# Squared values of the MLP stored unsplit, split on load by ScalarE and GpSimd

## The chip, the cores and the metric

The kernel runs on one core of a Trainium2 chip. The metric is the device time of one execution in microseconds (us), lower is better; runs of one kernel are summarised by their median. The kernel before takes 2271.26 us (median of 3 runs, 2271.02 to 2272.39).

## The reference

One decoder block on an input of 1024 rows by 1024 columns in float32: two token mixers (dilated attention and retention), an output projection, and at the end the MLP that this change is about:

```python
    xn2 = rmsnorm(x, norm2_g[l])
    x = x + jnp.square(jax.nn.relu(xn2 @ w_up[l])) @ w_down[l]
```

`w_up` is 1024 x 4096 and `w_down` 4096 x 1024. All of it is float32.

## The kernel before

**Split products.** Each float32 operand of a matmul is split into a high part, a rounded copy of type fp32r that ScalarE writes (`activation` Copy), and a low part, the rest (`tensor_tensor` subtract on VectorE). The helper `split` does both; its two lines are L318 and L319. Each product is then three matmuls: high by high, high by low, low by high. The function `group` (line L223) issues them all. Only TensorE's order is written out by hand; the order on the other engines comes from a planner that puts instructions in the order in which it expects them to be ready, with expected durations of its own, and each engine then runs its list strictly in order. All transfers are issued from SyncE's queue (SP), in order too.

**Strassen.** Both MLP products use Strassen's scheme in Winograd's form: seven products N1 to N7 in place of eight. TensorE sums them in PSUM banks: bank `a` holds N1 and then N2 added on top, bank `b` holds minus N1 (copied there by ScalarE, L387 and L1163) and then N6, N7 and N4, bank `d` holds N5 and then N3. Between two products of one bank, some engine reads the intermediate sum, and the next product of that bank has to wait for it.

**Up projection.** 16 units j (256 columns of `w_up` each), seven products of 12 matmuls (128x128 by 512 columns) per unit, in the order of `strassen_order`: N6, N5, N1 of unit j+2, N7, N2 of unit j+2, N4, N3. After N7, ScalarE copies bank `b` out (L395), then N4 goes on in that bank. The class `Weights` keeps a fixed list of weight splits; a raw weight buffer is loaded again (L176) as soon as the last split that reads it is done. Each result passes Relu and Square on ScalarE (L1110, L1111). The four squared quarters (`q11`, `q12`, `u3`, `u2`) and four sums of them that VectorE makes (L1117) are the seven left operands of the down projection. `put_operand` splits each of them into `hs` (high and low, 128 x 2 x 512) and stores both parts to `h_d` in DRAM (L1127), 512 KB each.

**Down projection.** 8 chunks c (512 rows of `w_down`) by 4 row blocks t make 32 units u. `load_rows(u)` loads the unit's seven operands, already split, into one of three places that served the up projection (`OP7["N1"]`, `["N5"]`, `["N3"]`): 896 KB of high parts and 896 KB of low parts (L1143). `down(u, name)` is one product of 6 matmuls. The order within a unit is N6, N5, N1 of unit u+1, N7, N2 of unit u+1, N3, N4; after that `load_rows(u + 3)`. VectorE adds or subtracts each sum to the output rows `Y` (L1171). The seven weight operands of the next chunk are made and split while a chunk runs (L153 are the sums on VectorE), most of them around a change of chunk, since their buffers come free there.

**The seam.** The last unit of the up projection overlaps the first two products of the down projection, written by hand:

```python
            if j == NU - 1:
                if name == "N1":
                    load_rows(0)
...
                if name == "N5":
                    load_rows(1)
                if name == "N7":
                    down(0, "N1")
                if name == "N4":
                    down(0, "N2")
                if name == "N3":
                    load_rows(2)
```

Lines and names that come up later: L223 all matmuls (`mm`, `ms` are the PSUM tiles, `xh`, `xl` the high and low operand, `wh`, `wl` those of the weights), L318 and L319 the splits, L1127 the stores of `h_d`, L1143 the row loads, L852 and L332 GpSimd's few small powers in earlier stages.

Of the kernel before, what the change touches and what calls it, by code (L numbers as in the profile page):

```python
# [17 lines left out]
P = 128  # L18
S = 1024
D = 1024  # L20
# [248 lines left out]
def hybrid_block(ctx: ExitStack, tc: tile.TileContext, a: dict, out: bass.AP):  # L269
# [26 lines left out]
    h_d = dram.tile([FF // 512, 2, 4, P, 7, 2, P], F, name="h_d")  # L296
# [60 lines left out]
    for nb in range(2):  # L357
        for u in range(4):
# [6 lines left out]
                  {"N1": "y1a", "N2": "y1b", "N3": "y1c", "N5": 3, "N7": "w1a", "N6": "w1b", "N4": "w1c"}])  # L365
# [720 lines left out]
    with ExitStack() as ph:  # L1086
        up_pool, early, sumst = None, [], ExitStack()
        unit = {}

        def temps():  # L1090

            nonlocal up_pool
            if up_pool is None:
                assert pipe.slot > last_turn
                norm2.close()
                y0 = pool(sumst, "y0", 1)
                Y.update((r, y0.tile([P, D], F, name=f"Y{r}")) for r in (0, 4))
                up_pool = pool(ph, "p26", 2)
            return up_pool

        def result(j, f, cs, src):
# [13 lines left out]
            if q == "u2":  # L1115
                for name, x, y in (("N5", "u3", "u2"), ("N7", "u2", "q11"), ("N6", "q11", "u3"), ("N3", "q12", "q11")):
                    nc.vector.tensor_tensor(held[j, x], held[j, x], held[j, y], op=OP.add)  # L1117
                    put_operand(j, name, held[j, x])
# [3 lines left out]
        def put_operand(j, name, x):  # L1122

            hs = temps().tile([P, 2, 512], R, name="hs", bufs=4)
            split(hs[:, 0], hs[:, 1], x)
            dst = h_d[j // 2, :, :, :, DOWN.index(name), j % 2]
            nc.sync.dma_start(dst.rearrange("h t p q -> p (h t) q"),  # L1127
                              hs.rearrange("p h (t q) -> p (h t) q", q=P).bitcast(F))
# [6 lines left out]

        def load_rows(u):

            if u < len(units):
                c, t = units[u]
                rows[u] = []  # L1140
                for i, x in enumerate(OP7[("N1", "N5", "N3")[u % 3]]):
                    x = x.rearrange("p a b -> p (a b)")[:, :7 * 2 * P]
                    nc.sync.dma_start(x.bitcast(F), h_d[c, i, t].rearrange("p o k q -> p (o k q)"))  # L1143
                    rows[u].append(x.rearrange("p (o k q) -> p o k q", o=7, k=2))

        def down(u, name):
# [9 lines left out]
            xh, xl = rows[u]  # L1156
# [19 lines left out]

        for j, name in strassen_order(NU):
            product("up", j, name, unit, OP7, temps, result)
            if j == NU - 1:
                if name == "N1":  # L1180
                    load_rows(0)
                if name == "N2":
                    parts = [x.rearrange("p a b -> p (a b)") for x in OP7[name]]
                    for i, part in enumerate("ab"):
                        W.places["n2" + part] = [x[:, 1024 * i:1024 * i + 1024] for x in parts]
                    W.free(("place", "n2"))
                if name == "N5":
                    load_rows(1)
                if name == "N7":
                    down(0, "N1")  # L1190
                if name == "N4":
                    down(0, "N2")
                if name == "N3":
                    load_rows(2)
# [3 lines left out]
        Y.update((r, y1.tile([P, D], F, name=f"Y{r}")) for r in (1, 5, 3, 7, 2, 6))  # L1198
        for x in "abc":
            W.places["y1" + x] = [y1.tile([P, UW], R, name=f"y1{x}{i}") for i in "hl"]  # L1200
# [3 lines left out]
    with ExitStack() as ph:  # L1204
# [5 lines left out]
        for u in range(len(units)):  # L1210
            for name, later in (("N6", False), ("N5", False), ("N1", True), ("N7", False), ("N2", True),
# [3 lines left out]
            load_rows(u + 3)  # L1215
# [107 lines left out]
```

## Time and profile before

| | |
|---|---|
| time, median of 3 runs | 2271.26 us |
| profiled execution, its own time | 2274.39 us |
| its span, first to last instruction | 2272.6 us |
| granted TensorE clock, mean | 0.996 |
| TensorE busy | 2233.6 us, 98% |
| VectorE, ScalarE, GpSimd busy | 59%, 44%, 5% |
| up projection | about 1639 to 1950 us of the span |
| down projection | about 1950 us to the end |
| `h_d` traffic: stores; row loads | 112 of 512 KB; 64 of 896 KB |

In the views below, PE is TensorE, DVE VectorE, ACT ScalarE, POOL GpSimd, SP SyncE's queue. A list of waits says which engine and line waited for which, then the total us, the number of times and the longest. A row of the timeline gives start, duration, engine, line, operation, `out<-in` by the program's names, and in brackets the idle time before it with what ended it. A row of a group gives count, busy us, mean ns of one, and the idle time before. The chain of waits is the chain of work that ended last, followed back to what released each step. Matmuls overlap, so their pace is read from start to start, not from their durations.

### The profile page before, as it was taken

The page shows a single profiled execution, that of the slowest core. Times are in us where ns is not written, and L with a number is a line of the kernel's source. Part 1 is how long each engine was busy: PE and PEld are TensorE (multiplying, and loading weights), DVE is VectorE, ACT ScalarE, POOL GpSimd, SP SyncE. Part 2 cuts the span into 40 slices and gives each one's busy share as a digit, 9 for nine tenths or more (in the row PEclk, how much of TensorE's full clock was granted, in tenths as well). Part 3 has the DMA queues.
Part 4 walks back from the last instruction along what each step waited for, and adds up shares of the span by engine and source line. Part 5 has one row for each costly group of instructions (what it writes and reads, how often), then busy time and mean ns, then how long its engine had stood idle before and what let it go on. Part 6 is the DMA issues. An engine that isn't in the chain of part 4 may idle for free.

```text
span 2272.6 us, 29996 instructions
## 1 busy us (share of the span) xinstructions
PE 2233.6 (98%) x10868; PEld 1911.3 (84%) x10868; DVE 1338.5 (59%) x2580; ACT 992.0 (44%) x2182; POOL 103.3 (5%) x148
## 2 busy tenths in 40 slices
PE   8999999999999999999999999999999999799999
PEld 7999999998888888888888878888787777688887
DVE  6444545455544445558676752363877777777874
ACT  6444435345433333345455633122567667532220
POOL 1111111110000000000000000000000000000000
PEclk9999999999999999999999999999999999899999
DMA  4313132323233333363433385554278888967665
GB/s 148 98 52 107 62 94 86 90 85 98 84 111 109 109 109 112 105 185 119 119 121 95 120 286 181 167 162 161 89 219 239 244 237 265 335 252 287 252 226 201
DMA packets 288805, 353.53 MB, mean 156 GB/s; under 512 B 14609, under 2 KB 215441, under 8 KB 288658
## 3 DMA queue, kind: packets, MB, share of 16 engines
q1 hardware_dynamic: 288658, 351.63, 48.4%
q8 instruction: 85, 1.39, 0.3%
q14 instruction: 62, 0.51, 0.1%
HBM read 229.84 MB, written 121.73 MB: 155 GB/s over the span
## 4 chain that ended last, share of the span: by engine, by line
PE 78%; DVE 8%; DMA 5%; ACT 5%; issue 3%; POOL 0%; SPq 0%; POOLq 0%; DVEq 0%; ACTq 0%
PE mm L223 52%; PE ms L223 20%; DVE wl L319 2%; DMA raw<-in_w_up 2%; PE ms L603 1%; PE ms L583 1%; ACT wh L318 1%; PE tr L659 1%; DVE Y L1171 1%; DVE hs L319 1%; DVE xl L319 1%; PE ms L596 1%; DVE raw L153 1%; ACT u L1110 1%; PE ms L819 1%
## 5 line engine op out<-in xcount | busy, mean ns | idle before, releaser
L223 PE MATMUL mm<-wh,xh 128*128 128x384 f32 (+1 forms) x1280 | 503.4, 393 | 9.3 <-DMA xh<-h_d 9.3
L319 DVE TENSOR_TENSOR wl<-raw,wh 128x1024 fp32r<-128x1024 f32 (+2 forms) x274 | 296.4, 1088 | 303.8 <-ACT wh L318 302.9
L223 PE MATMUL mm<-wh,xl 128*128 128x384 f32 (+1 forms) x1280 | 460.4, 360 | 3.0 <-DVE xl L319 2.0
L223 PE MATMUL mm<-wl,xh 128*128 128x384 f32 (+1 forms) x1280 | 459.3, 359 | 0.0
L318 ACT ACTIVATE wh<-raw 128x1024 fp32r<-128x1024 f32 (+2 forms) x274 | 258.6, 950 | 322.3 <-PE ms L223 81.0
L223 PE MATMUL mm<-xl,wh 128*128 128x512 f32 x848 | 309.8, 390 | 1.7 <-DVE xl L319 1.7
L223 PE MATMUL mm<-xh,wh 128*128 128x512 f32 x848 | 310.3, 390 | 0.0
L223 PE MATMUL mm<-xh,wl 128*128 128x512 f32 x720 | 280.6, 390 | 0.0
L223 PEld LDWEIGHTS mm<-wh,xh 128*128 128x128 f32 x1280 | 242.2, 189 | 30.3 <-ACT w1ch L318 9.7
L223 PEld LDWEIGHTS mm<-wh,xl 128*128 128x128 f32 x1280 | 241.2, 188 | 26.1 <-DVE xl L319 3.0
L223 PEld LDWEIGHTS mm<-wl,xh 128*128 128x128 f32 x1280 | 243.1, 190 | 19.3 <-DVE wl L319 0.4
L223 PE MATMUL ms<-xh,wh 128*128 128x512 f32 x604 | 239.7, 397 | 7.3 <-ACT u L395 4.5
L223 PE MATMUL ms<-xh,wl 128*128 128x512 f32 x604 | 235.4, 390 | 0.0
L223 PE MATMUL ms<-xl,wh 128*128 128x512 f32 x604 | 235.2, 389 | 0.0
L223 PEld LDWEIGHTS mm<-xl,wh 128*128 128x128 f32 x848 | 159.6, 188 | 35.0 <-DVE xl L319 2.1
L223 PEld LDWEIGHTS mm<-xh,wh 128*128 128x128 f32 x848 | 159.6, 188 | 33.2
L223 PEld LDWEIGHTS mm<-xh,wl 128*128 128x128 f32 x720 | 135.4, 188 | 28.2
L223 PEld LDWEIGHTS ms<-xh,wh 128*128 128x128 f32 x604 | 113.5, 188 | 36.9 <-ACT u L395 10.4
L223 PEld LDWEIGHTS ms<-xh,wl 128*128 128x128 f32 x604 | 113.3, 188 | 23.9
L223 PEld LDWEIGHTS ms<-xl,wh 128*128 128x128 f32 x604 | 113.5, 188 | 22.2
L590 ACT ACTIVATE pr<-s,acc 128x128 f32<-128x128 f32 (+1 forms) x96 | 43.1, 449 | 148.7 <-DVE acc L588 124.0
L1171 DVE TENSOR_TENSOR Y<-Y,ms 128x512 f32<-128x512 f32 x88 | 60.3, 685 | 62.5 <-PE ms L223 62.3
(257 smaller groups left out, 3295.0 us busy)
## 6 DMA issues: line engine op xcount, KB each, us to landing
h_d<-hs SPq DMA_DIRECT2D x112, 512.0 KB, 5.1
xh<-h_d SPq DMA_DIRECT2D x32, 896.0 KB, 5.0
xl<-h_d SPq DMA_DIRECT2D x32, 896.0 KB, 7.2
raw<-in_w_att SPq DMA_DIRECT2D x48, 384.0 KB, 3.9
raw<-in_w_up SPq DMA_DIRECT2D x32, 512.0 KB, 4.2
raw<-in_w_down SPq DMA_DIRECT2D x32, 512.0 KB, 5.5
sg_d<-sg SPq DMA_DIRECT2D x32, 256.0 KB, 2.0
raw<-in_w_rqk_q SPq DMA_DIRECT2D x16, 512.0 KB, 3.7
```

The costliest lines, as they stand in the source:

```text
L153: self.nc.vector.tensor_tensor(self.raw[r], self.raw[r], self.raw[other], op=op)
L223: self.nc.tensor.matmul(ps, x, y, start=start, stop=stop, skip_group_check=not first)
L318: nc.scalar.activation(dst_h, src, AF.Copy)
L319: nc.vector.tensor_tensor(dst_l, src, dst_h.bitcast(F), op=OP.subtract)
L583: nc.tensor.matmul(sp[:, :n], qT[:, b * P:(b + 1) * P], kT[:, k0:k0 + n], start=True, stop=True)
L590: nc.scalar.activation(st["p"][:, :n], s[:, :n], AF.Exp, bias=acc[:, b, DH:DH + 1], accum_out=acc[:, b, DH + 1:DH + 2])
L596: nc.tensor.transpose(tp[:, j * P:(j + 1) * P], st["p"][:, j * P:(j + 1) * P], ident)
L603: nc.tensor.matmul(po[:, :DH], st["t"][:, j * P:(j + 1) * P], V[:, k0 // P + j, :], start=(j == 0), stop=(j == nk - 1))
L659: nc.tensor.transpose(pt[:, j, :], qk[:, j, :], ident)
L819: nc.tensor.matmul(sp[:, :P], kT[:, f], qT[:, f], start=(f == 0), stop=(f == 1))
L1110: nc.scalar.activation(r, src, AF.Relu)
L1171: nc.vector.tensor_tensor(Y[r][:, ns], Y[r][:, ns], ps, op=op)
```

## The change

`h_d` keeps each operand once, unsplit, in float32. `put_operand` stores the squared value or sum as it is, 256 KB; the sums of a unit go into tiles of their own (`s`, four buffers), so that the value being stored isn't overwritten. `hs` and its splits are gone.

The down projection loads a unit's seven operands raw, 896 KB in all, into one of two halves of the place `OP7["N1"]` (`raws`). `split_rows` splits them: ScalarE copies the high parts in one instruction, GpSimd subtracts the low parts in slices of 256 columns, one per operand. The first two operands (N1, N2), which a unit needs one unit ahead, are split on their own into the small pool `rn`; the other five go into one of two places (`row_places`), `OP7["N5"]` and a new pair of tiles in the pool `y1`. `prepare(u)`, now at the start of unit u, splits the five operands of unit u+1, issues the load of unit u+3 and splits the pair of unit u+2. At the seam the rows of units 0 and 1 are asked for after (15, N1) and those of unit 2 after (15, N5). The weight operands N2 and N3 of odd chunks move from `y1` to `OP7["N3"]`, which the rows no longer use.

```diff
--- before.py
+++ after.py
@@ -293,7 +293,7 @@
     pb_d = dram.tile([KT, P, S], F, name="pb_d")
     v_d = dram.tile([HEADS, S, DH], F, name="v_d")
 
-    h_d = dram.tile([FF // 512, 2, 4, P, 7, 2, P], F, name="h_d")
+    h_d = dram.tile([FF // 512, 4, P, 7, 2, P], F, name="h_d")
     y_d = dram.tile([S, D], F, name="y_d")
 
     def slot_of(from_):
@@ -362,7 +362,7 @@
     NC = FF // 512
     W.add_chunks("dn", [[a["w_down"][c, i] for i in range(4)] for c in range(NC)],
                  [{"N1": 0, "N2": 1, "N3": 2, "N5": "n2a", "N7": "n2b", "N6": 5, "N4": 4},
-                  {"N1": "y1a", "N2": "y1b", "N3": "y1c", "N5": 3, "N7": "w1a", "N6": "w1b", "N4": "w1c"}])
+                  {"N1": "y1a", "N2": "n3a", "N3": "n3b", "N5": 3, "N7": "w1a", "N6": "w1b", "N4": "w1c"}])
     pipe = Pipe(nc)
 
     def product(tag, j, name, unit, operands, pu, result):
@@ -1084,7 +1084,7 @@
 
 
     with ExitStack() as ph:
-        up_pool, early, sumst = None, [], ExitStack()
+        up_pool, first_two, early, sumst = None, None, [], ExitStack()
         unit = {}
 
         def temps():
@@ -1095,6 +1095,8 @@
                 norm2.close()
                 y0 = pool(sumst, "y0", 1)
                 Y.update((r, y0.tile([P, D], F, name=f"Y{r}")) for r in (0, 4))
+                nonlocal first_two
+                first_two = pool(sumst, "rn", 2)
                 up_pool = pool(ph, "p26", 2)
             return up_pool
 
@@ -1113,19 +1115,17 @@
             if q != "u2":
                 put_operand(j, {"q11": "N1", "q12": "N2", "u3": "N4"}[q], r)
             if q == "u2":
-                for name, x, y in (("N5", "u3", "u2"), ("N7", "u2", "q11"), ("N6", "q11", "u3"), ("N3", "q12", "q11")):
-                    nc.vector.tensor_tensor(held[j, x], held[j, x], held[j, y], op=OP.add)
-                    put_operand(j, name, held[j, x])
+                for name, x, y in (("N5", "u3", "u2"), ("N7", "u2", "q11"), ("N6", "q11", "N5"), ("N3", "q12", "N6")):
+                    held[j, name] = temps().tile([P, 512], F, name="s", bufs=4)
+                    nc.vector.tensor_tensor(held[j, name], held[j, x], held[j, y], op=OP.add)
+                    put_operand(j, name, held[j, name])
 
         held = {}
 
         def put_operand(j, name, x):
 
-            hs = temps().tile([P, 2, 512], R, name="hs", bufs=4)
-            split(hs[:, 0], hs[:, 1], x)
-            dst = h_d[j // 2, :, :, :, DOWN.index(name), j % 2]
-            nc.sync.dma_start(dst.rearrange("h t p q -> p (h t) q"),
-                              hs.rearrange("p h (t q) -> p (h t) q", q=P).bitcast(F))
+            dst = h_d[j // 2, :, :, DOWN.index(name), j % 2]
+            nc.sync.dma_start(dst.rearrange("t p q -> p t q"), x.rearrange("p (t q) -> p t q", q=P))
 
 
         units = [(c, t) for c in range(NC) for t in range(4)]
@@ -1133,15 +1133,38 @@
         sums = {}
         Y = {}
 
+        def flat(name):
+            return [x.rearrange("p a b -> p (a b)") for x in OP7[name]]
+
+        raws = [x[:, :7 * 2 * P].bitcast(F) for x in flat("N1")]
+        row_places = [[x[:, :5 * 2 * P] for x in flat("N5")]]
+
         def load_rows(u):
 
             if u < len(units):
                 c, t = units[u]
-                rows[u] = []
-                for i, x in enumerate(OP7[("N1", "N5", "N3")[u % 3]]):
-                    x = x.rearrange("p a b -> p (a b)")[:, :7 * 2 * P]
-                    nc.sync.dma_start(x.bitcast(F), h_d[c, i, t].rearrange("p o k q -> p (o k q)"))
-                    rows[u].append(x.rearrange("p (o k q) -> p o k q", o=7, k=2))
+                nc.sync.dma_start(raws[u % 2], h_d[c, t].rearrange("p o k q -> p (o k q)"))
+
+        def split_rows(u, pair):
+
+            if u < len(units):
+                n = 2 if pair else 5
+                if pair:
+                    h, l = (first_two.tile([P, n * 2 * P], R, name=x) for x in ("rh", "rl"))
+                else:
+                    h, l = row_places[u % 2]
+                src = raws[u % 2][:, :512] if pair else raws[u % 2][:, 512:]
+                nc.scalar.activation(h, src, AF.Copy)
+                for i in range(n):
+                    cs = slice(2 * P * i, 2 * P * i + 2 * P)
+                    nc.gpsimd.tensor_tensor(l[:, cs], src[:, cs], h[:, cs].bitcast(F), op=OP.subtract)
+                rows[u, pair] = [x.rearrange("p (o k q) -> p o k q", o=n, k=2) for x in (h, l)]
+
+        def prepare(u):
+
+            split_rows(u + 1, False)
+            load_rows(u + 3)
+            split_rows(u + 2, True)
 
         def down(u, name):
 
@@ -1153,7 +1176,8 @@
                 b[bank] = mm.tile([P, 512], F, name="mm")
             o = DOWN.index(name)
             wh, wl = W["dn", c, name]
-            xh, xl = rows[u]
+            xh, xl = rows[u, o < 2]
+            o = o if o < 2 else o - 2
             pipe.step(b[bank], [(xh[:, o, k], xl[:, o, k], wh[:, 512 * k:512 * k + 512], wl[:, 512 * k:512 * k + 512])
                                 for k in range(2)], None, fresh)
             ps = b[bank]
@@ -1174,30 +1198,37 @@
             if t == 3:
                 W.free(("dn", c, name))
 
+        def weight_places(name, slot):
+
+            for i, part in enumerate("ab"):
+                W.places[name + part] = [x[:, 1024 * i:1024 * i + 1024] for x in flat(slot)]
+            W.free(("place", name))
+
         for j, name in strassen_order(NU):
             product("up", j, name, unit, OP7, temps, result)
-            if j == NU - 1:
-                if name == "N1":
-                    load_rows(0)
-                if name == "N2":
-                    parts = [x.rearrange("p a b -> p (a b)") for x in OP7[name]]
-                    for i, part in enumerate("ab"):
-                        W.places["n2" + part] = [x[:, 1024 * i:1024 * i + 1024] for x in parts]
-                    W.free(("place", "n2"))
-                if name == "N5":
-                    load_rows(1)
-                if name == "N7":
-                    down(0, "N1")
-                if name == "N4":
-                    down(0, "N2")
-                if name == "N3":
-                    load_rows(2)
+            if j < NU - 1:
+                continue
+            if name == "N1":
+                load_rows(0)
+                load_rows(1)
+                split_rows(0, True)
+            if name == "N2":
+                weight_places("n2", name)
+            if name == "N5":
+                prepare(-1)
+            if name == "N7":
+                down(0, "N1")
+            if name == "N4":
+                down(0, "N2")
+            if name == "N3":
+                weight_places("n3", name)
         exts.close()
         y1 = pool(sumst, "y1", 1, "right")
 
-        Y.update((r, y1.tile([P, D], F, name=f"Y{r}")) for r in (1, 5, 3, 7, 2, 6))
-        for x in "abc":
-            W.places["y1" + x] = [y1.tile([P, UW], R, name=f"y1{x}{i}") for i in "hl"]
+        Y.update((r, y1.tile([P, D], F, name=f"Y{r}")) for r in (1, 5))
+        row_places.append([y1.tile([P, 5 * 2 * P], R, name=f"r{x}1") for x in "hl"])
+        W.places["y1a"] = [y1.tile([P, UW], R, name=f"y1a{x}") for x in "hl"]
+        Y.update((r, y1.tile([P, D], F, name=f"Y{r}")) for r in (3, 7, 2, 6))
         W.free(("place", "y1"))
 
 
@@ -1208,11 +1239,11 @@
         W.free(("place", "w1"))
         px = pool(ph, "px7", 2)
         for u in range(len(units)):
+            prepare(u)
             for name, later in (("N6", False), ("N5", False), ("N1", True), ("N7", False), ("N2", True),
                                 ("N3", False), ("N4", False)):
                 if u + later < len(units):
                     down(u + later, name)
-            load_rows(u + 3)
             c, t = units[u]
             if 2 <= c < 6 and t % 2 == 0:
 
```

## The prediction

> **What bounds the kernel now.** I read the page's busy line first, then the windows table by stage, TensorE's list of waits, the timeline of each wait, and last the queues that the change touches.
>
> ```profile
> PE 2233.6 (98%) x10868; PEld 1911.3 (84%) x10868; DVE 1338.5 (59%) x2580; ACT 992.0 (44%) x2182; POOL 103.3 (5%) x148
> ...
> 1639.00:1950.00 311.00, 306.06 (x1325) 248.00 (x1323) 240.61 (x333) 213.41 (x350) 0.00 (x0) 1.00 0.82 239
> 1950.00:1976.00 26.00, 15.10 (x59) 11.62 (x60) 22.39 (x26) 16.39 (x24) 0.00 (x0) 0.81 1.00 336
> 1976.00:2111.00 135.00, 134.76 (x585) 110.48 (x584) 92.73 (x113) 37.03 (x46) 0.00 (x0) 0.99 0.74 272
> 2066.00:2089.00 23.00, 22.95 (x102) 18.61 (x101) 22.68 (x27) 7.53 (x9) 0.00 (x0) 1.00 0.73 256
> ```
>
> The window rows give length, then busy time and count of PE, PEld, DVE, ACT, POOL, then granted clock, DMA share, GB/s. TensorE (PE) sets the time nearly everywhere, and the change leaves its 10868 matmuls and their order alone. So only TensorE's waits can move the time: those that go, and those that come. The first row is the up projection, the second the seam, the third steady down projection, the last one chunk boundary in it. GpSimd (POOL) does nothing in all four. TensorE's waits here:
>
> ```profile
> PE mm L223 <- DMA xh<-h_d: 9.3, 1, 9.3
> ...
> PE ms L223 <- ACT u L395: 4.5, 13, 0.5
> ...
> PE ms L223 <- DVE wl L319: 1.1, 1, 1.1
> PE mm L223 <- DMA xl<-h_d: 0.9, 1, 0.9
> ```
>
> The columns are total us, times, longest. Two sit at the seam and are rows that arrive late, one at the seam is a weight split, and one returns 13 times in the up projection.
>
> **The seam: what goes.**
>
> ```profile
> 1963.17 0.69 DVE hs L319
> ...
> 1964.61 1.56 SPq L1143
> ...
> 1966.22 8.16 DMA xl<-h_d
> 1962.60 0.39 PE L223 MATMUL mm<-xh,xl 128*128 128x512 f32 x1
> 1972.32 0.76 PE L223 MATMUL mm<-wh,xh 128*128 128x512 f32 x1 [9.33 <-DMA xh<-h_d]
> ...
> 1974.42 0.80 PE L223 MATMUL mm<-wh,xl 128*128 128x512 f32 x1 [0.92 <-DMA xl<-h_d]
> ...
> 1979.71 0.42 PE L223 MATMUL mm<-wh,xl 128*128 128x512 f32 x1
> 2037.10 2.72 PE mm L223 x12
> ```
>
> The last row gives the undisturbed pace, 2.72/12 = 0.227 us a matmul. From 1962.60 to 1979.71 TensorE starts 15 matmuls in 17.11 us; at pace they take 3.40. The seam's row wait costs 13.7 us, not the 10.2 of the wait rows: behind the gap the matmuls ran at 0.43 spacing, and the granted clock of that window is 0.81. The cause stands in the first three rows (chain of waits): the rows of unit 2 are issued on SP's queue at 1964.61, behind the last stores, which wait for the low-part split at 1963.17 on VectorE; then the transfer takes 8.16 us with the DMA engines at a share of 1.00.
>
> The change moves that load: unit 2's rows are asked for after the (15,N5) product, in front of the last four stores, and wait only for GpSimd to have read unit 0's rows. It also halves the bytes:
>
> ```profile
> h_d<-hs SPq DMA_DIRECT2D x112, 512.0 KB, 5.1
> xh<-h_d SPq DMA_DIRECT2D x32, 896.0 KB, 5.0
> xl<-h_d SPq DMA_DIRECT2D x32, 896.0 KB, 7.2
> ```
>
> The 112 stores become 256 KB each, the 64 row loads 32: 28.7 + 28.7 MB fewer. I take the 13.7 us as gone. What is late next is the split of the rows: unit 1's five operands need a place that an earlier product frees, one ScalarE copy and five GpSimd subtractions, all by the start of unit 1, and unit 3's load waits for them. I charge 1 us (0 to 7 in the range). The weight split of N6, 1.1 us of wait and some 0.4 of slow restart, goes too, since VectorE loses its `hs` subtractions right ahead of it: 1.5.
>
> **The up projection: what goes.**
>
> ```profile
> 1669.35 4.20 DMA raw<-in_w_up
> ...
> 1885.75 4.28 DMA raw<-in_w_up
> 1884.51 1.22 DVE L319 TENSOR_TENSOR wl<-raw,wh 128x1024 fp32r<-128x1024 f32 x1
> 1890.06 2.01 ACT L318 ACTIVATE wh<-raw 128x1024 fp32r<-128x1024 f32 x2 [0.83 <-DMA raw<-in_w_up]
> 1891.97 0.58 ACT L395 ACTIVATE u<-ms 128x512 f32<-128x512 f32 x1
> 1892.60 0.50 PE L223 MATMUL ms<-xh,wh 128*128 128x512 f32 x1 [0.46 <-ACT u L395]
> L318 ACT ACTIVATE hs<-q 128x512 fp32r<-128x512 f32 x64 | 40.0, 625 | 33.7 <-DVE q L1117 29.9 <-DMA h_d<-hs 3.3
> L319 DVE TENSOR_TENSOR hs<-q,hs 128x512 fp32r<-128x512 f32 x64 | 43.8, 688 | 5.2 <-ACT hs L318 5.2
> ```
>
> The first two rows are eleven units apart: 19.67 us a unit, where 84 matmuls at pace take 19.04. So 0.63 a unit is lost, 8.2 over the 13. It is a loop: a weight buffer frees when VectorE's split ends (1885.73), its load lands 4.28 later, ScalarE, which stood idle 0.83 for it, makes two 1.0 us copies and only then the copy L395 that N4 needs. The change takes 7 `hs` copies (0.63) off ScalarE and 7 subtractions (0.69) off VectorE per unit, 4.4 and 4.8 us; at least one pair is in each round of the chain (about 1.2 us, twice the 0.63), and the DMA share falls from 0.82 by the halved stores. The four additions of a unit stay, only into tiles of their own. Bounds: nothing if the order of ScalarE keeps L395 behind a late load, 8.2 if the loop gets shorter than 19.04; I take 8.2 because the loop needs to shrink by only 3%.
>
> **The down projection: what comes.** Per unit of 42 matmuls (9.52 us): one ScalarE copy of 1280 columns and one of 512, and seven GpSimd subtractions of 128x256 (224 in all). ScalarE: 1024 columns take about 1.05 (a 1.05 to 1.06 row stands in the up group's 2.01 for two), 512 take 0.63, so 1280 about 1.3, with 0.63 makes 1.9 a unit; it is busy 37.03 of 135, so 27% becomes 47%. What is queued behind them is the copy of N1's sum, which N2 waits for one product (1.36 us) later:
>
> ```profile
> L1163 ACT ACTIVATE ms<-mm x30: 578/582/591, 1976.5 to 2256.6; 128x512 f32<-128x512 f32 x30
> ```
>
> That leaves 0.78 us. The long copy is free to run at the unit's start, 4 us earlier; the short one waits for rows that land about then. I charge nothing for it; if it collides, up to 0.5 us a unit.
>
> GpSimd's subtraction has no row. Nearest rows:
>
> ```profile
> L319 DVE TENSOR_TENSOR ql<-rqT,qh x28: 418/426/426, 1005.7 to 1288.6; 128x256 fp32r<-128x256 f32 x28
> L852 POOL TENSOR_TENSOR st<-st,half x32: 549/888/1522, 1015.3 to 1316.9; 128x1 f32<-128x1 f32 x32
> 1261.09 1.52 POOL L852 TENSOR_TENSOR st<-st,half 128x1 f32<-128x1 f32 x1 [10.24 <-DVE st L851]
> 1260.98 1.23 DVE L319 TENSOR_TENSOR xl<-oar,xh 128x1024 fp32r<-128x1024 f32 x1
> ```
>
> VectorE does the same shape in 0.42: the low end. A GpSimd instruction alone has 0.55 even for one column (a power); with VectorE's 0.42 for the columns that is 0.97: the high end. I take T = 0.7, between the two. Seven make 4.9 us of 9.52, so GpSimd isn't the bound below T = 1.36. The Trainium skill (GPSIMD Engine Reference, "Performance versus the Vector engine") gives 4497 ns for a two-tensor add of 2048 columns, about twice VectorE; an eighth of it, 0.56, is an estimate from that page, and no run here shows it; the sum by it would be 2249.
>
> The last two rows show more: 549 ns became 1.52 us where GpSimd started just behind a VectorE operation with two SBUF inputs, and it ended 0.4 after that one. GpSimd waited about 0.97 for VectorE. So the two take turns. At a chunk boundary VectorE has no slack: 22.68 busy of 23.00 in the window row, with twelve two-input operations between these two,
>
> ```profile
> 2066.43 1.22 DVE L319 TENSOR_TENSOR wl<-raw,wh 128x1024 fp32r<-128x1024 f32 x1
> ...
> 2085.75 1.22 DVE L319 TENSOR_TENSOR wl<-raw,wh 128x1024 fp32r<-128x1024 f32 x1
> 2086.88 0.68 DVE L1171 TENSOR_TENSOR Y<-Y,ms 128x512 f32<-128x512 f32 x1
> 2087.48 0.68 DVE L1171 TENSOR_TENSOR Y<-Y,mm 128x512 f32<-128x512 f32 x1
> ```
>
> mostly one `Y` addition apart (0.60 from start to start; its other input is PSUM). A GpSimd turn fits into that 0.60; what is longer delays VectorE, by T - 0.6 each time if VectorE must also wait for GpSimd, which no row shows. The `Y` additions behind are what lets TensorE reuse the bank two products (2.72 us) later. At 0.7 it is 12 x 0.1 = 1.2 a boundary, of which I let half through, and I add 0.4 for rows that GpSimd, with about one turn per VectorE turn, delivers late: 1.0, seven boundaries, 7 us. Ends: nothing (or 2 us of gain, the 0.3 a boundary that TensorE loses there today), and 12 x 0.37 x 7 = 31 at T = 0.97.
>
> SP's queue gets a new wait: the load for unit u+3 waits for GpSimd's subtractions, and weight loads stand behind it. They have a chunk (38 us) of time, so I cost it at nothing; if GpSimd were a whole unit late, weights would be too. Weights placed elsewhere cost nothing: the new place is free after (15,N3), and chunk 1 needs it 28 us later.
>
> **Sum.** -13.7 - 1.5 + 1 - 8.2 + 7 = -15.4. The profiled execution took 2274.39 (span 2272.6 and 1.8 around it), so 2259.0 there; the median of the runs is 3.1 lower, 2271.26, so 2255.9: 2256.
>
> **Rivals.**
> - *Turn-taking decides (slower).* Place: the chunk boundaries. Price: 12 x (T - 0.6) each. From 3.2 a boundary, T = 0.87, the 22.4 of gains are gone; at 0.97 the time is 2271.3 - 22.4 + 31 = 2280. For it: VectorE's full window, and GpSimd's stretched rows. Against: the order alternates with PSUM additions. The Trainium skill (SBUF — State Buffer, "SBUF: two separate sides") says the pair of ports is held exclusively for the whole instruction by a two-SBUF-input VectorE operation or by GpSimd, and the loser blocks; the trace agrees for GpSimd (0.55 to 1.52), the other direction is unseen.
> - *GpSimd is the bound.* Above T = 1.36 each of 31 units lasts 7T: at 1.8, 12.6, so 2271 - 22 + 31 x 3.1 = 2345. Against: its fixed 0.55 and VectorE's rate.
> - *The up projection's loop stays*, since ScalarE's order still puts late weights ahead of L395: 2256 + 8 = 2264.
> - *A new wait at the seam*: unit 1's split or unit 3's rows late by 7 us more: 2263. For it: ScalarE is busy 16.39 of 26 there and VectorE 22.39.
>
> **How the numbers follow.** Forecast 0.55 (own range 2249 to 2264), turns 0.17, GpSimd bound 0.05, loop 0.12, seam 0.11. A measurement can tell about 0.2%, 4.5 us: faster is below 2266.7, slower above 2275.8. Faster: 0.53 + 0.02 + 0.10 + 0.09 = 0.74; same 0.09; slower 0.17. The range: 2246 (nothing lost at boundaries, 2 gained) to 2276, which leaves out most of the turns' end and the GpSimd bound.
>
> **What would show it.** Right: no wait for `h_d` rows at the seam and a granted clock near 1 there; L395 gone from TensorE's waits; 128x256 GpSimd operations near 0.7; DMA share near 0.5 in both projections. Wrong: GpSimd operations over 0.9, TensorE waits on `Y` additions or on the low rows at the boundaries, or ScalarE's L1163 behind a row copy.

## The result, and the profile after

The kernel after takes 2334.01 us (median of 4 runs, 2331.58 to 2337.01) against 2271.82 us of the kernel before in the same comparison (4 runs, 2271.02 to 2273.3): ratio 1.0274, 95% interval 1.0256 to 1.0291. It is slower by 62 us, where 2256 was forecast. The profiled execution took 2336.11 us, its span is 2334.3, which is 61.7 more than the span before.

The windows by stage of the kernel after, in the columns explained in the prediction (the up projection at its pace, up projection with the start of the seam, the window in which the seam of the kernel before lay, and the down projection in two parts):

```profile
1650.00:1930.00 280.00, 280.00 (x1236) 231.56 (x1235) 164.71 (x211) 147.52 (x226) 5.99 (x5) 1.00 0.54 161
1639.00:1950.00 311.00, 307.91 (x1348) 253.69 (x1347) 188.50 (x236) 167.84 (x257) 19.82 (x16) 0.99 0.54 160
1950.00:1976.00 26.00, 24.15 (x105) 19.29 (x104) 14.04 (x16) 14.87 (x22) 13.02 (x16) 0.99 0.72 248
1976.00:2111.00 135.00, 113.75 (x450) 91.05 (x449) 83.69 (x95) 45.63 (x55) 75.28 (x74) 0.90 0.35 127
2111.00:2334.00 223.00, 188.08 (x756) 148.63 (x754) 121.73 (x148) 59.87 (x71) 108.58 (x119) 0.93 0.32 111
```

The up projection is what was forecast: TensorE is busy in all of the 280 us. In the window where the seam of the kernel before lay it is busy for 24.15 of 26 instead of 15.10, but the seam has moved: the down projection now starts at 1939.38 instead of 1949.08, and its unit 0 takes 15.27 us where 9.52 is the pace. The large loss is in the fourth and fifth rows, where before TensorE had 134.76 of 135. No engine is the bound there: VectorE works 83.69 of 135, GpSimd 75.28, ScalarE 45.63, and the DMA share has fallen from 0.74 to 0.35. Low busy shares everywhere with a TensorE that waits are the mark of a chain in which things happen one after another.

By starts of the matmuls, the 61.7 us split so: the down projection starts 9.7 earlier (8.4 of the up projection, 1.3 from ahead of it), units 0 and 1 take 24.79 instead of 34.33 (9.5 gained), and from unit 2 to the last matmul it takes 365.96 instead of 285.01 (81.0 lost). Units 2 to 30 take 12.39 us on the mean instead of 9.60.

The list of waits of the kernel after from 1950 us to the end shows the chain (us in total, times, longest):

```profile
POOL rl L1160 <- ACT rh L1157: 154.0, 34, 6.7
ACT rh L1157 <- DMA xl<-h_d: 113.0, 15, 9.3
ACT rh L1157 <- DMA xh<-h_d: 71.3, 12, 9.2
...
PE ms L223 <- DVE Y L1195: 42.8, 10, 8.3
DVE xl L319 <- ACT xh L318: 32.4, 9, 7.5
...
PE mm L223 <- ACT ms L1187: 10.9, 8, 3.4
```

and SP's own list over the same stretch:

```profile
SPq L1146 <- POOL rl L1160: 83.9, 14, 8.0
...
SPq L1146 <- POOL xl L1160: 64.7, 14, 6.8
```

Read together they close a ring: SP's row load (L1146) waits for GpSimd's subtraction, ScalarE's copy (L1157) waits for the load, GpSimd's subtraction (L1160) waits for the copy. The chain of waits in that stretch goes round it (start, us, what; in the loads `xh` and `xl` are the raw buffers of even and odd units, by the names of the tiles whose places they took; as outputs of L1160, `xl` and `rl` are places of low parts):

```profile
1997.94 5.00 DMA xl<-h_d
...
2003.05 0.64 ACT rh L1157
...
2003.76 1.15 POOL rl L1160 x2
...
2005.16 3.53 POOL xl L1160 x5
...
2008.70 4.47 DMA xh<-h_d
...
2013.28 0.64 ACT rh L1157
...
2013.99 1.15 POOL rl L1160 x2
...
2015.38 5.55 POOL rl L1160 x5
...
2020.95 4.44 DMA xl<-h_d
```

From load to load it is 10.76 and 12.25 us: 4.5 to 5.0 of transfer, 0.64 of copy, 1.4 for the pair's two subtractions, and 3.5 (undisturbed) or 5.5 (beside VectorE) for five subtractions. TensorE needs new rows each 9.52. The five subtractions at 2005.16 read the other buffer (`xl<-xh`), whose rows had lain there all along: in the order that the planner made, GpSimd does the pair of unit u+2 first and then the five of unit u+1, while the next load may start only when those five are done. So the five wait for a load that they don't need. From the seventh row load on, each one starts only after the one before it has landed, 10.2 to 16.7 us after that one's start, 12.7 on the mean: about the 12.39 of a unit.

What the ring does to TensorE goes over two more queues. The timeline of the kernel after around one boundary:

```profile
2025.49 0.63 ACT L1157 ACTIVATE rh<-xl 128x512 fp32r<-128x512 f32 x1 [8.96 <-DMA xl<-h_d]
2026.03 1.04 ACT L318 ACTIVATE xh<-raw 128x1024 fp32r<-128x1024 f32 x1
...
2027.11 1.59 DVE L319 TENSOR_TENSOR xl<-raw,xh 128x1024 fp32r<-128x1024 f32 x1 [6.78 <-ACT xh L318]
2028.62 0.68 DVE L1195 TENSOR_TENSOR Y<-Y,mm 128x512 f32<-128x512 f32 x1
...
2030.54 0.80 PE L223 MATMUL ms<-w1ah,rh 128*128 128x512 f32 x1 [6.16 <-DVE Y L1195]
```

ScalarE stands 8.96 us at the copy of the late rows; behind it in its list is a weight split, VectorE stands 6.78 for that with a `Y` addition behind it, and TensorE waits 6.16 for the bank which that addition should have read. The rows that were late weren't even due: TensorE is at N7 (`w1ah`) of a unit, and this pair is first used by the N1 that runs in the next unit.

### The profile page after: what moved, and what is told of

It reads as the page before. It is cut to its first block, busy times and chain, and to the rows that moved or that the text cites. A ratio compares the mean times of both kernels' runs of the same rounds, so it can differ in the third digit from the quotient of the medians.

```text
span 2334.3 us, 30051 instructions
## 1 busy us (share of the span) xinstructions
PE 2254.4 (97%) x10868; PEld 1925.9 (83%) x10868; DVE 1286.5 (55%) x2468; ACT 987.3 (42%) x2134; POOL 318.8 (14%) x372
## 3 DMA queue, kind: packets, MB, share of 16 engines
q8 instruction: 85, 1.39, 0.2%
## 5 line engine op out<-in xcount | busy, mean ns | idle before, releaser
L319 DVE TENSOR_TENSOR wl<-raw,wh 128x1024 fp32r<-128x1024 f32 (+2 forms) x274 | 302.6, 1107 | 420.0 <-ACT wh L318 419.1
L223 PE MATMUL mm<-wh,xh 128*128 128x384 f32 (+1 forms) x1184 | 465.1, 393 | 0.7 <-DVE Y L1195 0.7
L223 PE MATMUL mm<-wh,xl 128*128 128x384 f32 (+1 forms) x1184 | 422.2, 357 | 2.2 <-DVE xl L319 2.2
L223 PE MATMUL mm<-wl,xh 128*128 128x384 f32 (+1 forms) x1184 | 421.0, 356 | 0.0
L223 PEld LDWEIGHTS mm<-wh,xl 128*128 128x128 f32 x1184 | 222.5, 188 | 20.8 <-DVE xl L319 3.1
L223 PEld LDWEIGHTS mm<-wh,xh 128*128 128x128 f32 x1184 | 223.7, 189 | 18.1 <-DVE Y L1195 1.6
L223 PEld LDWEIGHTS mm<-wl,xh 128*128 128x128 f32 x1184 | 224.5, 190 | 15.5 <-DVE wl L319 0.4
L1160 POOL TENSOR_TENSOR rl<-xl,rh 128x256 fp32r<-128x256 f32 x112 | 119.3, 1094 | 99.7 <-ACT rh L1157 93.8
L852 POOL TENSOR_TENSOR st<-st,half 128x1 f32<-128x1 f32 x32 | 25.0, 780 | 766.2 <-DMA at<-acc_d 489.1
```

Of the source, the lines that this page charges most:

```text
L223: self.nc.tensor.matmul(ps, x, y, start=start, stop=stop, skip_group_check=not first)
L319: nc.vector.tensor_tensor(dst_l, src, dst_h.bitcast(F), op=OP.subtract)
L852: nc.gpsimd.tensor_tensor(st[:, 9:10], st[:, 8:9], half[:, 0:1], op=OP.pow)
L1160: nc.gpsimd.tensor_tensor(l[:, cs], src[:, cs], h[:, cs].bitcast(F), op=OP.subtract)
```

## The experiments

Names: theory A is the ring made by the order of pair and five. The labels below are those of the runs; where an edit is "on" another experiment, that one is kept. What was open after the first two was why they gained 8 to 11 us and not 15.

**1. Only the order** (e1_five_first): the pair's copy and subtractions keep the place in which the program writes them, behind the five.

```diff
-                nc.scalar.activation(h, src, AF.Copy)
+                keep = tc.keep_in_program_order if pair and u > 0 else lambda x: x
+                keep(nc.scalar.activation(h, src, AF.Copy))
...
-                    nc.gpsimd.tensor_tensor(l[:, cs], src[:, cs], h[:, cs].bitcast(F), op=OP.subtract)
+                    keep(nc.gpsimd.tensor_tensor(l[:, cs], src[:, cs], h[:, cs].bitcast(F), op=OP.subtract))
```

> Edit: ScalarE's copy and GpSimd's subtractions of the pair of unit u+2 are kept behind those of the five operands of unit u+1, as prepare(u) writes them; the planner had put the pair in front. Nothing else changes. Theory A (the order closes a serial loop: five subtractions, load of 4.5 us, pair copy 0.64, pair subtractions 1.4, next five, together 10.3 us or more against 9.52 of a unit): the loop opens, GpSimd has 4.9 us of work per unit, the down projection goes back to about 9.5 us a unit with some loss at chunk boundaries, time 2247 to 2262. Theory B (GpSimd and VectorE taking turns at the port is what slows the down projection, about 11.6 us a unit): the order is no matter, time stays above 2300. Theory C (both, about half each): 2280 to 2300.

Measured: 2265.42 us (2264.01 to 2268.33, 5 runs) against 2274.21 of before, ratio 0.9963 (0.9948 to 0.9977). The same instructions in another order are 69 us faster than the kernel after by the medians (71 by the ratios to the kernel before), and faster than the kernel before. The expected top was passed by 3 us; the kernel before stood 2.4 higher in this comparison too. TensorE's waits from 1935 us on:

```profile
PE ms L223 <- ACT Y L1194: 3.2, 1, 3.2
PE mm L223 <- ACT ms L1188: 3.1, 5, 1.6
PE ms L223 <- DVE Y L1196: 1.1, 3, 0.5
PE mm L223 <- DVE Y L1196: 0.4, 1, 0.4
```

7.8 us in place of 57.4 in the kernel after (the two rows above, 3.0 at the seam and 0.7). The units between the boundaries are at 9.52 again; the seven boundaries lose 10.0 us together (before: 2.3). The 3.1 us of the second row are N2 waiting for ScalarE's copy of N1's sum. The longest of these waits, 1.6 us, has this on ScalarE in front of it:

```profile
2148.95 0.63 ACT L1158 ACTIVATE rh<-xh 128x512 fp32r<-128x512 f32 x1 [3.95 <-DMA xh<-h_d]
2149.49 1.04 ACT L318 ACTIVATE wh<-raw 128x1024 fp32r<-128x1024 f32 x1
2150.44 0.58 ACT L1188 ACTIVATE ms<-mm 128x512 f32<-128x512 f32 x1
```

The pair's copy stands for its rows, and the copy that TensorE needs stands behind it.

**2. The ring opened at another place** (e2_pair_own_raw): the planner's order stays, but the pair's rows are loaded by a transfer of their own into free columns of `OP7["N5"]`, so that the load of the five waits for no pair.

```diff
-                nc.sync.dma_start(raws[u % 2], h_d[c, t].rearrange("p o k q -> p (o k q)"))
+                rows_d = h_d[c, t].rearrange("p o k q -> p (o k q)")
+                if u < 2:
+                    nc.sync.dma_start(raws[u % 2], rows_d)
+                else:
+                    nc.sync.dma_start(raws[u % 2][:, 512:], rows_d[:, 512:])
+        pair_raws = [x[:, 5 * 2 * P:7 * 2 * P].bitcast(F) for x in flat("N5")]
+        def load_pair(u):
...
+                nc.sync.dma_start(pair_raws[u % 2], h_d[c, t].rearrange("p o k q -> p (o k q)")[:, :512])
...
```

> Edit: the order of the changed kernel is left to the planner, but from unit 2 on the pair's rows are loaded into places of their own (256 KB and 640 KB loads instead of one of 896 KB), so the pair's load doesn't wait for the five subtractions of two units before. Theory A, the loop through the shared raw buffer is the cause and not the order by itself: about the same gain as the kept order, 2247 to 2265. If the order by itself costs (ScalarE stands at the pair with weight splits behind it whatever its rows' place is): 2290 or more. Theory B (turns at the port): above 2300.

Measured: 2263.05 us (2262.61 to 2263.88, 4 runs), ratio 0.9951 (0.9936 to 0.9966), the fastest full version of the study. Both ways of opening the ring make 69 to 71 us of the loss go, so it was the ring, and not GpSimd's amount of work, which is the same in both. What is left here: unit 0 takes 17.27, and the seven boundaries lose 6.9 together (before: 2.3).

**3. The same work without GpSimd** (e4_low_on_vector): on 1, the low parts are made by VectorE.

```diff
-                    keep(nc.gpsimd.tensor_tensor(l[:, cs], src[:, cs], h[:, cs].bitcast(F), op=OP.subtract))
+                    keep(nc.vector.tensor_tensor(l[:, cs], src[:, cs], h[:, cs].bitcast(F), op=OP.subtract))
```

> Edit: kept order, and the low parts of the rows are subtracted by VectorE instead of GpSimd (seven of 0.42 us per unit, 2.9 us more). Theory A: no loop either, but VectorE, at 69% of the down projection before, goes to about 97% there; the chunk boundaries, where it was full, lose about 20 us of VectorE work over some 2.4 units, 5 to 7 us a boundary: 2285 to 2310. Theory B (GpSimd at the port is the cost): better than with GpSimd, under 2280.

Measured: 2323.55 us (1 run), worse than the range. TensorE's wait:

```profile
PE ms L223 <- DVE Y L1196: 49.3, 25, 6.9
```

VectorE takes 0.42 for the shape, but has no room at the boundaries: those units take 16.8 to 19.1 us. GpSimd is the better place for these subtractions by 58 us, with its turns.

**4. Where the up projection's gain comes from** (e6_store_twice): on 1, every operand is stored twice, so that the stores move as much as before.

```diff
+            dst = h2_d[j // 2, :, :, DOWN.index(name), j % 2]
+            nc.sync.dma_start(dst.rearrange("t p q -> p t q"), x.rearrange("p (t q) -> p t q", q=P))
```

> Edit: kept order, and each squared operand is stored a second time to another place in DRAM that nothing reads, so the up projection has the store traffic of the kernel before (58.7 MB), without the splits. It asks what freed the up projection of its 0.63 us a unit. If it was the DMA load: the wait of N4 for L395 comes back, 19.6 us a unit, about 8 us more than with the kept order alone. If it was the splits taken off ScalarE and VectorE: the up projection stays at 19.04 a unit and the time within 3 us of the kept order alone.

Measured: 2264.8 us (1 run). The windows row of the up projection:

```profile
1650.00:1930.00 280.00, 280.00 (x1237) 231.94 (x1236) 160.93 (x207) 146.09 (x224) 3.97 (x4) 1.00 0.88 253
```

TensorE is busy throughout with a DMA share of 0.88, above the 0.84 of the kernel before in the same window. So the 8 us come from the splits that ScalarE and VectorE no longer do, not from the halved stores.

**5. The seam's load later** (e7_seam_load_late): on 2, the rows of unit 2 are asked for after (15, N3), so that ScalarE's weight split, which stood 3.90 us for a weight load behind them, isn't held.

```diff
-            load_rows(u + 3)
+            if u >= 0:
+                load_rows(u + 3)
...
             if name == "N3":
+                load_rows(2)
```

> Edit: pair rows in places of their own, as before, and at the seam the load of unit 2's five operands is issued after the (15, N3) product instead of after (15, N5), so that the weight loads of w_down no longer stand behind it on SP's queue while it waits for GpSimd. With the pair places alone unit 0 of the down projection lasted 17.3 us (7.7 too long): ScalarE stood 3.9 us at a weight split for a load issued at 1937 behind that row load. Theory: that queue is the cause; 5 to 7 us of it go, ratio to the kernel before about 0.992 to 0.993. Rival: the weight load is late by itself (its buffer comes free late, 6 us of transfer) and ScalarE's order keeps Y copies behind it: the seam stays within 2 us of 7.7, ratio 0.995.

Measured: 2264.78 us (2262.53 to 2266.39, 6 runs), ratio 0.9959 (0.9947 to 0.9971); unit 0 still 17.43. The rival's figure came, but not by its mechanism: ScalarE no longer stands for that weight load, and TensorE's longest wait is now one of 4.6 us for VectorE. The timeline of VectorE there:

```profile
1942.63 1.76 DVE L319 TENSOR_TENSOR xl<-raw,xh 128x1024 fp32r<-128x1024 f32 x1
1944.32 1.74 DVE L319 TENSOR_TENSOR wl<-raw,wh 128x1024 fp32r<-128x1024 f32 x1
1945.99 1.22 DVE L1120 TENSOR_TENSOR s<-u,u 128x512 f32<-128x512 f32 x1
...
1949.42 1.75 DVE L319 TENSOR_TENSOR xl<-raw,xh 128x1024 fp32r<-128x1024 f32 x1
...
1952.22 1.74 DVE L153 TENSOR_TENSOR raw<-raw,raw 128x1024 f32<-128x1024 f32 x1
1953.89 0.68 DVE L1212 TENSOR_TENSOR Y<-Y,ms 128x512 f32<-128x512 f32 x1
```

1.22 us became 1.74 to 1.76, and the 0.68 of an addition of two SBUF tiles (L1120) became 1.22; the `Y` addition, with an input in PSUM, still takes 0.68. Eight such operations at some 0.53 are 4.3 us, about the 4.6 that TensorE waited for that `Y`. VectorE does wait for GpSimd.

**6. Shorter turns** (e8_slices_128): on 5, GpSimd's slices are 128 columns.

```diff
-                for i in range(n):
-                    cs = slice(2 * P * i, 2 * P * i + 2 * P)
+                for i in range(2 * n):
+                    cs = slice(P * i, P * i + P)
```

> Edit: as the kernel with the late seam load, and GpSimd's subtractions are 128 columns wide instead of 256, 14 per unit. It asks how long a turn at the port may be. A 256-wide one takes 0.71 us alone. If the cost goes by columns, 128 take about 0.4, a turn fits into the 0.60 of one Y addition, and the loss at a chunk boundary falls from about 1.1 us to the 0.4 of the kernel before: 4 to 5 us faster than the late seam load alone. If a fixed part of about 0.55 (the one-column power) carries it, 128 take about 0.63, 14 make 8.8 of 9.52 us, rows come late and it is 5 us or more slower.

Measured: 2267.98 us (2264.71 to 2270.77, 9 runs), ratio 0.9972 (0.9963 to 0.9981): 3 us slower than 5 by the medians, though the two intervals overlap, and the units at the boundaries take 10.33 to 10.97, about as in 5. Neither expectation holds in full: shorter turns don't help, and a slice's median of 0.46 us against 0.74 for twice the columns means a quarter more GpSimd time.

**7. Longer turns** (e3_full_width): on 1, one subtraction over 1280 or 512 columns.

```diff
-                for i in range(n):
-                    cs = slice(2 * P * i, 2 * P * i + 2 * P)
+                for cs in (slice(0, n * 2 * P),):
```

> Edit: the kept order (pair behind five), and GpSimd subtracts the five operands in one instruction of 1280 columns and the pair in one of 512. The work is the same. If VectorE waits for the whole GpSimd instruction, a two-input operation of VectorE at a chunk boundary can stand about 3 us instead of 0.7, the Y additions behind it too, and a boundary loses 2 to 4 us more than with the kept order alone: 2280 to 2295. If the two share the port access by access, turns are no matter: within 4 us of the kept order alone (2265).

Measured: 2290.53 us (1 run), as expected. Groups of VectorE from 1950 us to the end (count, busy us, mean ns):

```profile
L1195 DVE TENSOR_TENSOR Y<-Y,ms 128x512 f32<-128x512 f32 x88 | 60.1, 683 | 60.7 <-PE ms L223 60.6
...
L153 DVE TENSOR_TENSOR raw<-raw,raw 128x1024 f32<-128x1024 f32 x26 | 54.1, 2080 | 0.1
```

The weight sums with two SBUF inputs go from 1.22 to 2.08 on the mean, and the additions with a PSUM input stay at 0.68. One such sum beside the GpSimd subtraction that it meets:

```profile
2029.92 3.33 POOL L1160 TENSOR_TENSOR rl<-xl,rh 128x1280 fp32r<-128x1280 f32 x1 [4.61 <-ACT rh L1158]
2030.97 3.36 DVE L153 TENSOR_TENSOR raw<-raw,raw 128x1024 f32<-128x1024 f32 x1
```

The subtraction ends at 2033.25 and the sum 1.08 us later, about the 1.22 that it takes alone. So VectorE's operation stood for nearly all the rest of GpSimd's: a turn lasts as long as the GpSimd instruction does.

**8 and 9. The first chunks in another order.** e11_chunk1_behind, on 2, pins the weight work of chunk 1 behind unit 0 on ScalarE and VectorE; e12_all_behind, on 8, also puts the row loads at the end of a unit on SP, those of unit 2 and the pair of unit 3 after (15, N3), and chunk 2's weights behind unit 3. The lines of e11 that place the weight work of chunk 1:

```diff
+            if u == 0:
+                W.behind = tc.keep_in_program_order
+                W.free(("place", "y1"))
+                W.behind = None
```

> Edit: pair rows in places of their own (load of unit 2 back where the changed kernel has it), and the weight splits and sums of chunk 1 are kept behind unit 0's copies and additions on ScalarE and VectorE; the planner had put them ahead, 30 us before chunk 1 needs them. Moving the row load on SP's queue had not helped: ScalarE no longer stood, but VectorE then ran without a pause from 1937 to 1957, its two-input operations at 1.74 instead of 1.22 us beside GpSimd, and TensorE waited 4.6 us for a Y addition behind them; unit 0 lasted 17.4 us. Theory: the order of VectorE and ScalarE at the seam, with chunk 1's weights in front of the additions, is the cause, and unit 0 falls to 9.5 to 12.5 us: 5 to 8 us, ratio 0.992 to 0.993, 2256 to 2259 where the kernel before takes 2274. Rival: VectorE has too much to do at the seam in any order (additions of the last up unit, chunk 0's weights, turns with GpSimd): unit 0 stays above 15 us, or unit 1 to 3 take what unit 0 gives, ratio 0.995.

> Edit: the kernel with chunk 1 kept behind, and two more: the rows' loads are issued at the end of a unit, behind that unit's weight loads on SP's queue, and chunk 2's weights are taken up only after unit 3, behind the copies of the first chunk's sums. With chunk 1 alone kept behind, unit 0 fell from 17.3 to 9.5 us, but unit 3 rose to 17.8: ScalarE stood 4.8 us at chunk 2's first weight split, for a load issued at 1971.1 behind a row load that waited for GpSimd, with copies of sums behind it. Theory: each time it is a load on SP's queue behind a row load, and a split that waits for it ahead of more urgent work; with both orders mended the first four units lose less than 4 us together (they lost 11 us with the kernel before's own seam aside) and the time is 6 to 8 us below the last kernel: ratio 0.993 to 0.994. Rival: VectorE is short of time over the first two chunks whatever the order, and the wait moves to units 4 to 8: ratio 0.996 as before.

Measured: 2265.55 us (2264.0 to 2265.79, 5 runs; ratio 0.9964, 0.995 to 0.9978) and 2265.11 (2263.24 to 2268.12, 5 runs; 0.9961, 0.9948 to 0.9975). Both rivals had the time about right; that VectorE is short of time in any order, their reason, isn't shown. In 8 unit 0 is at 9.52 and unit 3 at 17.79; in 9 units 1 and 4 lose 4.4 and 5.7. The loss of 8 to 10 us moves with the order and doesn't go. For 8, ScalarE's timeline names the new place, a wait for a weight load:

```profile
1977.66 1.06 ACT L321 ACTIVATE wh<-raw 128x1024 fp32r<-128x1024 f32 x1 [4.83 <-DMA raw<-in_w_down]
```

**10. No turns at all** (e13_no_low_rows): on 2, without GpSimd's work; the products of the rows' low parts are left out of the sum.

```diff
-                for i in range(n):
-                    cs = slice(2 * P * i, 2 * P * i + 2 * P)
-                    nc.gpsimd.tensor_tensor(l[:, cs], src[:, cs], h[:, cs].bitcast(F), op=OP.subtract)
-                rows[u, pair] = [x.rearrange("p (o k q) -> p o k q", o=n, k=2) for x in (h, l)]
+                rows[u, pair] = [x.rearrange("p (o k q) -> p o k q", o=n, k=2) for x in (h, h)]
```

> The pair's own places as in e2_pair_own_raw; GpSimd's subtractions are left out, and the matmuls read the high parts of the rows in place of the low parts (so the low parts of the rows are left out of the sum); loads and ScalarE's copies stay. Theory (what is left to lose in the down projection is turns between GpSimd and VectorE): VectorE's 128x1024 operations go back to 1.22 us everywhere, the chunk boundaries lose 0.3 to 0.5 each in place of 1.06, units 0 and 1 lose under 4 us together in place of 8.1, and the time is 5 to 10 us under e2: ratio 0.991 to 0.993. Rival (it is the order of loads and copies on SP and ScalarE): units 0 and 1 still lose 7 or more, only the boundaries' 4 to 5 us go: ratio 0.993 to 0.9945. Second rival (turns cost nothing in the sum): within 2 us of e2, ratio 0.9942 or more.

Measured: 2255.44 us (2253.8 to 2259.09, 5 runs) against 2274.92, ratio 0.992 (0.9906 to 0.9934). That is 7 us of the time by the two ratios (0.0031 of 2274), as the first theory expected; unit 0 still loses 4.4, a little over its bound. TensorE's waits from 1930 us on, and one of VectorE's groups:

```profile
PE ms L223 <- ACT Y L1206: 2.5, 1, 2.5
PE mm L223 <- ACT ms L1200: 0.2, 1, 0.2
...
L153 DVE TENSOR_TENSOR raw<-raw,raw 128x1024 f32<-128x1024 f32 x27 | 33.0, 1221 | 0.1
```

Every wait on a `Y` addition of VectorE is gone, and the weight sums are at 1.22 (1.39 in 2). The boundaries lose 2.3 us together, as in the kernel before, in place of 6.9; units 0 and 1 lose 4.4 in place of 8.1, and of 2's longest wait at the seam half (2.5 of 5.5) is left. The run takes away a stage of the chain of row loads together with the turns, so it doesn't prove by itself that all 7 us are turns; VectorE's durations speak for most of the boundaries' part.

## Why the prediction was wrong

**The step that failed** is the one that cost SP's new wait at nothing ("They have a chunk (38 us) of time, so I cost it at nothing") together with ScalarE's short copy, which "waits for rows that land about then. I charge nothing for it". Two mistakes are in it. The wait was priced by the weight loads that stand behind it on SP, and not as a link: load, copy, subtractions and the next load share a buffer, so they are a ring, and a ring costs its whole length when that is over 9.52. And `prepare` was read as if the engines kept its written order, five before pair, although ScalarE's and GpSimd's order comes from the planner. With five first the next load doesn't wait for the one before it; with pair first each load waits for it, and the two rounds shown are 10.8 and 12.3 us long. Price: 69 us by the medians (experiment 1 against the kernel after), and the prediction's rows had its parts: 5.0 us for a load of 896 KB, 0.63 for the copy and 7 x 0.7 for GpSimd make 10.5.

**The rest of the sum, without the ring.** Experiment 1 has the order that the prediction read, five before pair. Its span is 9.8 us below that of the kernel before, where 15.4 was forecast: the down projection starts 8.1 earlier, units 0 and 1 gain 9.3 where 14.2 was forecast, and the boundaries lose 7.7 more (10.0 - 2.3) where 7 was charged. So the seam is the term that was mis-sized, by some 5 us. The nearness of 7.7 to 7 is in part luck: 3.1 of it are waits for the copy of N1's sum, and the two longest of these, 1.6 and 0.8, come from the short copy that was charged at nothing.

**The rivals.** The forecast's bound T > 1.36 for GpSimd came from its busy time alone; no rival had it in a ring with the load. The rival that decided for slower, turns at the boundaries, gave 2280 from T = 0.97, and wasn't what happened: that loss exists, but is 4.6 us in experiment 2 and at most 7.7 in experiment 1.

**Right in mechanism and size.** The up projection: 19.04 us a unit, and L395 is no longer among TensorE's waits: 8.4 gained, 8.2 forecast, and for the reason given (experiment 4). TensorE no longer waits for `h_d` rows at the seam; the granted clock is 0.99 in the window of the old seam, but 0.89 from 1939 to 1955, where unit 0 now lies. A GpSimd subtraction of 128x256 costs 0.70 undisturbed, from this row of the timeline, where 0.7 was forecast:

```profile
2005.16 3.52 POOL L1160 TENSOR_TENSOR xl<-xh 128x256 fp32r<-128x256 f32 x5
```

The 0.7 was the middle of two distant bounds, 0.42 and 0.97, so that it fits is in part luck; over all 224 in the kernel after, with the waits for VectorE, the mean is 1.00. An eighth of the 4497 ns that the Trainium skill (GPSIMD Engine Reference, "Performance versus the Vector engine") gives for 2048 columns is an estimate of 0.56; the measurement decides.

**Right in mechanism, wrong in size.** The boundaries: 7 was charged, experiment 2 shows 6.9 - 2.3 = 4.6. The seam: what is late next was charged 1 us (0 to 7 allowed); in the kernel after and in experiment 1 units 0 and 1 lose 5.8 and 5.9, and in experiments 2, 5, 8 and 9 it is 8 to 10 us in the first five units (less the 0.5 of their boundary before). So 13.7 + 1.5 - 1 became 9.5 in the kernel after and about 7 in experiment 2 (34.33 - 27.12). With these sizes and without the ring the prediction's sum would be -8.4 - 7.2 + 4.6 = -11.0, and experiment 2 measured 0.9951, or -11.1.

**The direction that no row showed.** VectorE waits for GpSimd as GpSimd does for VectorE: 1.22 to 1.74, and 3.36 in the row of experiment 7. The Trainium skill (SBUF — State Buffer, "SBUF: two separate sides") says that a VectorE operation with two SBUF inputs and GpSimd hold the ports exclusively, for the whole instruction; the trace now agrees in both directions.

**Left open.** About 4.4 us at the seam (2.5 by the list of waits) stay without any GpSimd work. Why the rest of the 8 to 10 us in the first chunks moves with each order, and doesn't fall between the units where VectorE has room, isn't settled; experiment 10 shows only that it goes with GpSimd's subtractions.

## What to carry to other kernels

Where a buffer is loaded again after an engine has read it, write down the ring (transfer, each engine's pass, the next transfer), add up its length in the order in which each engine's list really stands, and compare that with the period of the bound engine; busy shares say nothing about it. When an instruction that waits for a transfer is put into an in-order list, look at which earlier-ready work stands behind it, on this engine and on those that wait for this one. Fix the order of two operations by hand where one of them releases the next transfer and the other one waits for it.

## What the runs showed of the hardware

- A GpSimd subtraction has medians of 0.46 us for 128 columns and 0.74 for 256 (0.42 and 0.70 from start to start). A line through the two medians has 0.18 that doesn't depend on the columns, and 0.28 for each 128; it gives 1.30 for 512 columns and 2.98 for 1280, and experiment 7's medians are 1.31 and 2.96. VectorE's 0.42 for 256 is 0.6 of the 0.70.
- Beside GpSimd, VectorE's operations with two SBUF inputs show longer durations (1.22 to 1.74, 0.68 to 1.22, up to 3.96 beside subtractions of 1280 columns), and GpSimd's own grow from 0.74 to means of about 0.9 to 1.1; those with a PSUM input stay at 0.68.
- The granted clock is 0.90 and 0.93 in the two windows of the down projection in which the ring makes TensorE pause, and 1.00 in the first of them in experiments 1 and 2. Of the 81 us lost, the waits name 54; most of the rest is 141 matmuls that start 0.25 to 1 us apart (median 0.43) instead of 0.227, as those behind the wait at 2030.54 do: about 27 us.
